# Attention scores in 32-query blocks on four column groups of TensorE, in a two-layer decoder trunk

## The chip, the cores and the metric

The kernel runs on one core of one Trainium2 chip. The metric is device time in microseconds (us) of one execution. A core has TensorE (PE, matmuls, with PEld its weight loads), VectorE (DVE), ScalarE (ACT), GpSimd (POOL) and SyncE (SP); each takes its instructions in program order, and semaphores order them among each other. Matmuls write PSUM, eight banks of 128 partitions x 2 KB; the other engines work between PSUM and SBUF.

## What is computed

Two layers of a decoder over 256 tokens of width 2048, each a mixer and a gated feed-forward network. Layer 0 mixes by gMLP and HGRN2, layer 1 by forgetting attention with 16 heads of 128. The change lies in the attention. What it must compute:

```python
def mixer_c(h, w_in, b_f, q_gain, k_gain, w_out):
    q, k, v, g, f = jnp.split(h @ w_in, ...)
    q = rms_norm(q.reshape(shp), q_gain)
    k = rms_norm(k.reshape(shp), k_gain)
    log_f = jax.nn.log_sigmoid(f + b_f)
    c = jnp.cumsum(log_f, axis=1).transpose(0, 2, 1)
    scale = C_HEAD_DIM ** -0.5
    for blk in range(seq // ATTN_BLOCK):          # two blocks of 128 queries
        lo, hi = blk * ATTN_BLOCK, (blk + 1) * ATTN_BLOCK
        s = jnp.einsum('bthd,bshd->bhts', q[:, lo:hi], k[:, :hi]) * scale
        s = s + c[:, :, lo:hi, None] - c[:, :, None, :hi]
        causal = (lo + jnp.arange(ATTN_BLOCK))[:, None] >= jnp.arange(hi)[None, :]
        p = jax.nn.softmax(jnp.where(causal, s, -jnp.inf), axis=-1)
        outs.append(jnp.einsum('bhts,bshd->bthd', p, v[:, :hi]))
    o = jnp.concatenate(outs, axis=1).reshape(bsz, seq, D_MODEL) * jax.nn.sigmoid(g)
    return o @ w_out
```

## The kernel before

All weights are streamed from HBM once, 484 MB in all. Every projection multiplies in split precision: a weight tile w of 128 x 1024 is loaded by SP's queue (L189), ACT rounds it to wh (L176), DVE takes the rest wl = w - wh (L177), and PE does three matmuls with 512 columns for each 128 x 512 part: L302 (wh), L303 (wl), L304 (wh with the low half of the activations) in the token-major projections, L321 to L323 in the feature-major ones. One tile feeds twelve matmuls. Four w, three wh and three wl buffers let the loads and halves run ahead. One call of tick() for each weight tile lets small generators (attend, gate, moves and so on) put their instructions between the projection's; a scheduler in the build then settles the order on each engine.

The attention's projections run in four groups of four heads: q, k and v of a group are three passes of project_tok over 16 parts of 128 features. The outputs of q and k are copied out of PSUM by ACT (z, L1051), squared and summed by DVE (junk L394, ss L395, then the reciprocal root: rm L386, a logarithm and an exponential on ACT L99, rt L389 to L391), scaled (L1059), transposed in 32 x 32 blocks by DVE (L334) and put in place by 16 DMAs of 32 KB, eight on SP's queue and eight on POOL's (L341, turn<-tmp).

Each pair of heads then goes through attend. ACT scales q and k into qk (L967). PE makes the scores of each head into one PSUM bank (L977, L978): queries 0 to 127 against keys 0 to 127, queries 128 to 255 against all 256; both are float32 matmuls, and what lies above the diagonal is computed and then masked. DVE adds the sums of the forget gates (ct by query, cb by key; L984, L986) and the mask cst (L988) and takes the maximum (L993); ACT takes the exponential and its sum (L99). DVE transposes the result in 32 x 32 blocks into ptmp (L1002), POOL's queue moves 16 blocks to pt (L1011), PE multiplies by v (L1023 to L1025) and ACT copies the two halves of the output to o, divided by the sums (L1027). At the end gate multiplies o with the sigmoid of the last projection's output.

PSUM: four banks (pm) hold the projections, four (px, through bank()) everything else. A matmul whose output lies in 32 partitions that start at 0, 32, 64 or 96 uses one of four column groups of the array. Three other places of the kernel do this already: L676 and L716 in the HGRN2 mixer, and L903 and L907 in the forget gates.

Of the kernel before, what the change touches and what calls it, by code (L numbers as in the profile page):

```python
# [8 lines left out]
F32 = mybir.dt.float32  # L9
F32R = mybir.dt.float32r  # L10
U16 = mybir.dt.uint16
AF = mybir.ActivationFunctionType
ALU = mybir.AluOpType
AX = mybir.AxisListType

P = 128
S = 256
# [3 lines left out]
CH = 16  # L21
# [3 lines left out]
BLK = 32  # L25
# [20 lines left out]
K_ID, K_TRI, K_CM, K_REV = 0, 128, 256, 384  # L46
# [8 lines left out]
def tile_trunk(ctx: ExitStack, tc: tile.TileContext, x, pp_d, cst_d, mlev_d, msk_d,  # L55
               w_v, w_f, w_g, w_i, w_q, w_u, w_abo, w_cf, w_cqkv, w_cg, w_co, w_up, w_dn, spw_d, spb_d, out):
    nc = tc.nc
    V, SC, PE = nc.vector, nc.scalar, nc.tensor
# [9 lines left out]
    def nm(base):  # L68
        count[0] += 1
        return f"{base}_{count[0]}"  # L70
# [3 lines left out]
    for c0, n in ((0, 1), (1, 1), (2, 2), (4, 2), (6, 2), (8, 4), (12, 4)):  # L74
        t = cp.tile([P, n, S], F32, tag=f"x{c0}", name=f"x{c0}")
# [4 lines left out]
    cst = cp.tile([P, NK], F32, tag="cst", name="cst")  # L80
# [30 lines left out]
    def turned(ap):  # L111

        return view(ap, 0, (1, 2), (2, P))

    def bank():
        return psum["pool"].tile([P, 512], F32, tag="px", name=nm("px"), bufs=psum["banks"])

    def banks(stack, n):

        psum.update(pool=stack.enter_context(tc.tile_pool(name=nm("px"), bufs=1, space=bass.MemoryType.PSUM)), banks=n)  # L120
        return psum["pool"]
# [243 lines left out]
    def held(r, last="wh"):  # L365

        tc.add_manual_dep(r.ins, deep[last].ins.name, order, reason="not before")
# [104 lines left out]
    def mixer_ab(norm):  # L472
        es = ExitStack()
        hp = es.enter_context(tc.tile_pool(name="hp", bufs=1))
# [161 lines left out]
        for j in range(2):  # L636
            ps = project_four(w_f[4 * j:4 * j + 4], A, KT)
# [3 lines left out]
            t = hp.tile([P, 1024], F32, tag="o", name=nm("turn"), bufs=2)  # L641
# [152 lines left out]
        for h in range(NH):  # L794
# [6 lines left out]
            ps = project(w_q[h], A)  # L801
# [5 lines left out]
        for j in range(2):  # L807
            ps = project_four(w_g[4 * j:4 * j + 4], A, KT)
# [16 lines left out]
        for j in range(2):  # L825
            ps = project_four(w_u[4 * j:4 * j + 4], A, KT)
# [3 lines left out]
            t = hp.tile([P, 1024], F32, tag="tok", name=nm("turn"), bufs=2)  # L830
# [12 lines left out]
        def stretch(q, ks, **kw):  # L843
            return project_four(w_abo[4 * q:4 * q + 4], product, KT, ks=ks, **kw)

        ahead = None
        for q in range(4):
            if q == 0:

                ps = stretch(0, (0, 2, 4, 6, 8, 10), more=True)  # L850
                ahead = stretch(1, (0, 2, 4, 6), more=True)
                stretch(0, (12, 14), ps=ps)
            elif q == 1:
                ps = stretch(1, (8, 10, 12, 14), ps=ahead)
            else:
                ps = stretch(q, range(0, KT, 2))
# [4 lines left out]
                depth[0] = 2  # L861
            add_four(q, ps, z, tmp, dst, nxt, 2 if q in (1, 2) else 1, (nc.sync, nc.gpsimd) if q else (nc.gpsimd,))
        es.close()
        banks(ctx, 4)
        return nxt


    def mixer_c(norm):
        es = ExitStack()
        hp = es.enter_context(tc.tile_pool(name="cpool", bufs=1))  # L870
# [23 lines left out]

        ct = hp.tile([P, 2, 2 * CH], F32, tag="ct", name="ct")[..., 0:CH]
        cb = hp.tile([P, CH * S], F32, tag="big", name="cb", bufs=1).rearrange("p (h s) -> p h s", s=S)

        def forget():

            ps = pm.tile([P, 512], F32, tag="pm", name=nm("pm"))  # L900
            pr = bank()
            for g in range(4):
                PE.matmul(pr[BLK * g:BLK * (g + 1), 0:LANE], ones[:, 0:BLK], norm.acc[:, LANE * g:LANE * (g + 1)],  # L903
                          start=True, stop=True)
            for k in range(KT):
                r = k % 4 * BLK
                PE.matmul(ps[r:r + CH, 0:S], w2[:, k], xT[k], start=k < 4, stop=k >= KT - 4, skip_group_check=True)  # L907
            return ps, pr
# [38 lines left out]
        def columns(fc):  # L947
            ps = bank()
            for T in range(2):
                PE.transpose(ps[:, T * P:(T + 1) * P], fc[:, T * P:(T + 1) * P], ident)  # L950
            V.tensor_copy(ct, ps[:, 0:S].rearrange("p (t c) -> p t c", t=2)[..., 0:CH])

        left = [CH]
        os_ = []
# [3 lines left out]
        def attend(hs, q, k, v, o):  # L958

            while steps[0] < turn[0]:  # L960
                yield
            turn[0] = steps[0] + PAIR
            qks = []
            for h in hs:
                qk = hp.tile([P, 2, S], F32, tag="qk", name=nm("qk"), bufs=2)
                for j, (t, g) in enumerate(((q, gq), (k, pp[:, C_KN:C_KN + 1]))):
                    r = SC.activation(qk[:, j].rearrange("p (t n) -> p t n", t=2), turned(t[:, h % 4]), AF.Copy, scale=g)  # L967
                    if j == 0:
                        held(r)
                qks.append(qk)  # L970
            yield
            sc = hp.tile([P, 6, P], F32, tag="sc", name=nm("sc"), bufs=1)
            scf = sc.rearrange("p a b -> p (a b)")
            sps = []
            for qk in qks:
                sp = bank()
                PE.matmul(sp[:, 0:P], qk[:, 0, 0:P], qk[:, 1, 0:P], start=True, stop=True)  # L977
                PE.matmul(sp[:, P:3 * P], qk[:, 0, P:S], qk[:, 1], start=True, stop=True)  # L978
                sps.append(sp)
            sums = []  # L980
            for i, (h, sp) in enumerate(zip(hs, sps)):
                c0 = 3 * P * i
                parts = ((c0, c0 + P), (c0 + P, c0 + 3 * P))
                V.scalar_tensor_tensor(scf[:, c0:c0 + P], sp[:, 0:P], ct[:, 0, h:h + 1], cb[:, h, 0:P],  # L984
                                       ALU.add, ALU.subtract)
                V.scalar_tensor_tensor(scf[:, c0 + P:c0 + 3 * P], sp[:, P:3 * P], ct[:, 1, h:h + 1], cb[:, h],  # L986
                                       ALU.add, ALU.subtract)
                V.tensor_tensor(sc[:, 3 * i:3 * i + 3:2], sc[:, 3 * i:3 * i + 3:2],  # L988
                                cst[:, K_CM:K_CM + P].unsqueeze(1).to_broadcast([P, 2, P]), ALU.add)
                mxs = hp.tile([P, LANE], F32, tag="mxs", name=nm("mxs"), bufs=2)[:, 0:2]  # L990
                sms = hp.tile([P, LANE], F32, tag="sms", name=nm("sms"), bufs=4)[:, 0:2]
                for T, (a, b) in enumerate(parts):
                    V.tensor_reduce(mxs[:, T:T + 1], scf[:, a:b], AX.X, ALU.max, negate=True)  # L993
                for T, (a, b) in enumerate(parts):
                    act(scf[:, a:b], scf[:, a:b], AF.Exp, bias=mxs[:, T:T + 1], accum_out=sms[:, T:T + 1])
                sums.append(sms)
            yield
            yield
            tmp = hp.tile([P, 6 * P], F32, tag="ptmp", name=nm("ptmp"), bufs=1)
            for i, sms in enumerate(sums):  # L1000
                V.reciprocal(sms, sms)
                t = V.transpose(tmp.rearrange("p (b m i) -> p b m i", b=4, m=6)[:, :, 3 * i:3 * i + 3],  # L1002
                                sc[:, 3 * i:3 * i + 3].rearrange("p m (b j) -> p b m j", b=4))
                if i == 0:
                    held(t, "wl")
            yield
            n = 6 * BLK
            pt = hp.tile([P, 6, P], F32, tag="pt", name=nm("pt"), bufs=2)
            for a in range(4):
                for b in range(4):  # L1010
                    nc.gpsimd.dma_start(pt[BLK * b:BLK * (b + 1), :, BLK * a:BLK * (a + 1)],  # L1011
                                        tmp[BLK * a:BLK * (a + 1), b * n:(b + 1) * n]
                                        .rearrange("p (m r) -> p m r", m=6))
                if a == 1:
                    yield
            for _ in range(LAG - 1):
                yield
            for i, (h, sms) in enumerate(zip(hs, sums)):
                d0 = (h % 4) * P
                op = bank()  # L1020
                v0, v1 = (v[:, T, d0:d0 + P] for T in range(2))
                p0, p1, p2 = (pt[:, 3 * i + m] for m in range(3))
                PE.matmul(op[:, 0:P], p0, v0, start=True, stop=True)  # L1023
                PE.matmul(op[:, P:S], p1, v0, start=True, stop=False)  # L1024
                PE.matmul(op[:, P:S], p2, v1, start=False, stop=True)  # L1025
                for T in range(2):
                    SC.activation(o[:, T, d0:d0 + P], op[:, T * P:(T + 1) * P], AF.Copy, scale=sms[:, T:T + 1])  # L1027
                left[0] -= 1

        def piece(tag, bufs):  # L1030
            return hp.tile([P, 1024], F32, tag=tag, name=nm(tag), bufs=bufs).rearrange("p (t c) -> p t c", t=2)
# [7 lines left out]
        for g in range(CH // 4):  # L1039
            qkv = []  # L1040
            ss = hp.tile([P, 2, 2, LANE // 4], F32, tag="ss", name=nm("ss"), bufs=2)[..., 0:4]
            for j in range(3):
# [5 lines left out]
                ps = early[j] if g == 0 and j < 2 else project_tok(w_cqkv[j * (CH // 4) + g], norm)  # L1048
# [6 lines left out]
                if j < 2:  # L1055
# [5 lines left out]
                    t = piece("turn", 4)  # L1061
# [34 lines left out]
        for q in range(CH // 4):  # L1096
            ps = project_four(w_cg[4 * q:4 * q + 4], A, KT)
# [6 lines left out]
        for q in range(4):  # L1104
            ps = project_four(w_co[4 * q:4 * q + 4], yB, KT)
# [236 lines left out]
```

## Time and profile before

| | |
|---|---|
| median of 3 runs | 2280.98 us (2280.97 to 2282.70) |
| the profiled execution | 2282.31 us, of which its span is 2280.5 us |
| attention stage with its projections | about 1120 to 1430 us of the span, the first scores at 1165.9 |
| PE busy between 1160 and 1430 us | 269.1 of 270.0 us |
| DVE, ACT, POOL busy between 1160 and 1430 us | 179.7, 149.9, 104.1 us |
| granted TensorE clock | 0.999 of full speed |

How to read the rows of the profile that follow. In a timeline a row has the start in us, the duration in us, the engine, the source line, the operation and the tiles (out<-in), the shape, and xN for N equal instructions that follow each other, merged; the brackets at the end tell how long the engine was idle before and what ended that. A float32 matmul stands as two PE records. The duration of a PE record includes its way through the array, so the distance between two starts, not the duration, tells how long PE was held. In a row of one line's instructions the three durations are minimum, median and maximum in ns. In the view of waits a row has the total in us, the number of times and the longest.

### The profile page before, as it was taken

The numbers are of one execution on the slowest core, as the hardware profiler recorded it, in microseconds if no ns is written. First come the engines' busy times: TensorE is split into PE (matmuls) and PEld (weight loads), VectorE is DVE, ScalarE is ACT, GpSimd is POOL, SyncE is SP. The second block draws the span as 40 slices with busy tenths as digits, with TensorE's granted clock in tenths as the row PEclk, the third lists the DMA queues.
The fourth block names the chain that finished last, engine by engine and source line by source line (L and its number), as shares of the span: only waits on it lengthen the run. The fifth ranks groups of instructions, "written<-read, shape, count | busy, mean of one in ns | idle before, by whom it ended". The sixth has DMA issues, their size and how long they took to land.

```text
span 2280.5 us, 32327 instructions
## 1 busy us (share of the span) xinstructions
PE 2273.4 (100%) x10786; PEld 1886.7 (83%) x10786; DVE 1562.2 (69%) x2301; ACT 1302.3 (57%) x1946; POOL 436.8 (19%) x798
## 2 busy tenths in 40 slices
PE   9999999999999999999999999999999999999999
PEld 8888888888888888888888888888888888888887
DVE  8788767767467656766876675666776476667766
ACT  7677656656456445654555556655665465455642
POOL 0120231221012002211233343211211012012102
PEclk9999999999999999999999999999999999999999
DMA  8655777777567666776676667777776676666766
GB/s 287 203 167 166 215 204 230 243 215 232 189 211 223 202 206 194 234 218 190 212 232 216 205 195 219 203 225 230 228 223 211 192 224 205 220 204 203 232 200 178
DMA packets 492615, 483.60 MB, mean 212 GB/s; under 512 B 115136, under 2 KB 460240, under 8 KB 492320
## 3 DMA queue, kind: packets, MB, share of 16 engines
q1 hardware_dynamic: 465888, 453.27, 64.1%
q0 software_dynamic: 24832, 25.92, 4.9%
q10 hardware_dynamic: 1728, 2.35, 0.3%
q8 instruction: 84, 1.38, 0.3%
q14 instruction: 83, 0.68, 0.1%
HBM read 435.24 MB, written 2.11 MB: 192 GB/s over the span
## 4 chain that ended last, share of the span: by engine, by line
PE 99%; DMA 1%; DVE 0%; issue 0%; POOL 0%; ACT 0%; DVEq 0%; SPq 0%
PE pm L321 27%; PE pm L323 27%; PE pm L322 27%; PE pm L302 4%; PE pm L303 4%; PE pm L304 4%; PE pm L276 2%; PE pm L203 1%; PE pm L279 1%; PE pm L227 0%; DMA pt<-ptmp 0%; PE px L978 0%; PE lv L716 0%; POOL pt L1011 0%; PE px L1024 0%
## 5 line engine op out<-in xcount | busy, mean ns | idle before, releaser
L177 DVE TENSOR_TENSOR wl<-w,wh 128x1024 fp32r<-128x1024 f32 (+1 forms) x820 | 995.9, 1218 | 611.7 <-ACT wh L176 580.6
L176 ACT ACTIVATE wh<-w 128x1024 fp32r<-128x1024 f32 (+1 forms) x820 | 862.7, 1054 | 763.1 <-PE pm L323 572.5
L321 PE MATMUL pm<-wh,a 128*128 128x512 f32 x1728 | 674.3, 390 | 0.0
L322 PE MATMUL pm<-wl,a 128*128 128x512 f32 x1728 | 672.6, 389 | 0.0
L323 PE MATMUL pm<-wh,a 128*128 128x512 f32 x1728 | 672.5, 389 | 0.0
L341 POOL DMA_DIRECT2D zt<-tmp x413 | 223.6, 549 | 1201.6 <-DVE tmp L334 1152.7
L323 PEld LDWEIGHTS pm<-wh,a 128*128 128x128 f32 x1728 | 324.4, 188 | 67.5
L321 PEld LDWEIGHTS pm<-wh,a 128*128 128x128 f32 x1728 | 324.4, 188 | 67.3
L322 PEld LDWEIGHTS pm<-wl,a 128*128 128x128 f32 x1728 | 324.4, 188 | 67.1 <-DVE wl L177 0.2
L323 PE MATMUL pm<-wh,hid 128*128 128x512 f32 x688 | 267.7, 389 | 0.0
L322 PE MATMUL pm<-wl,hid 128*128 128x512 f32 x688 | 267.7, 389 | 0.0
L321 PE MATMUL pm<-wh,hid 128*128 128x512 f32 x688 | 267.7, 389 | 0.0
L302 PE MATMUL pm<-wh,a 128*128 128x512 f32 x416 | 164.7, 396 | 0.0
L303 PE MATMUL pm<-wl,a 128*128 128x512 f32 x416 | 162.4, 390 | 0.9 <-DVE wl L177 0.9
L304 PE MATMUL pm<-wh,a 128*128 128x512 f32 x416 | 162.1, 390 | 0.0
L322 PEld LDWEIGHTS pm<-wl,hid 128*128 128x128 f32 x688 | 129.1, 188 | 26.8
L321 PEld LDWEIGHTS pm<-wh,hid 128*128 128x128 f32 x688 | 129.1, 188 | 26.8
L323 PEld LDWEIGHTS pm<-wh,hid 128*128 128x128 f32 x688 | 129.1, 188 | 26.8
L341 POOL DMA_DIRECT2D turn<-tmp x160 | 86.8, 550 | 316.7 <-DVE tmp L334 237.1
L1146 ACT ACTIVATE conv<-zt,pp 128x256 f32<-128x256 f32 x176 | 95.9, 590 | 36.1 <-DMA zt<-tmp 25.5
L1147 DVE SCALAR_TENSOR_TENSOR conv<-zt,pp,conv 128x255 f32<-128x255 f32 x176 | 79.7, 479 | 28.0 <-ACT conv L1146 27.7
L334 DVE STREAM_TRANSPOSE tmp<-z 128x512 f32<-128x512 f32 x120 | 82.8, 703 | 17.0 <-ACT z L1132 16.4
(246 smaller groups left out, 2131.6 us busy)
## 6 DMA issues: line engine op xcount, KB each, us to landing
w<-in_w_up SPq DMA_DIRECT2D x352, 512.0 KB, 4.9
w<-in_w_dn SPq DMA_DIRECT2D x176, 512.0 KB, 4.9
w<-in_w_cqkv SPq DMA_DIRECT2D x96, 512.0 KB, 4.6
w<-in_w_abo SPq DMA_DIRECT2D x32, 512.0 KB, 4.5
w<-in_w_cg SPq DMA_DIRECT2D x32, 512.0 KB, 4.6
w<-in_w_co SPq DMA_DIRECT2D x32, 512.0 KB, 4.8
zt<-tmp SPq DMA_DIRECT2D x414, 32.0 KB, 2.3
zt<-tmp POOLq DMA_DIRECT2D x413, 32.0 KB, 2.2
```

What stands on the lines that cost most here:

```text
L176: r = deep["wh"] = SC.activation(wh, w, AF.Copy)
L177: deep["wl"] = V.tensor_tensor(wl, w, wh.bitcast(F32), ALU.subtract)
L302: PE.matmul(ps[T], ah, h, start=k + i == 0, stop=False)
L303: PE.matmul(ps[T], ah, l, start=False, stop=False)
L304: deep["last"] = PE.matmul(ps[T], al, h, start=False, stop=k + i == KT - 1)
L321: PE.matmul(ps[T], ah, h, start=not begun and k + i == ks[0], stop=False)
L322: PE.matmul(ps[T], ah, l, start=False, stop=False)
L323: deep["mm"] = deep["last"] = PE.matmul(ps[T], al, h, start=False, stop=not more and k + i == ks[-1] + 1)
L334: V.transpose(tmp.rearrange("p (b m i t) -> p b m i t", b=4, m=4, t=2)[:, :, :, :, T], src(T).rearrange("p (m b j) -> p b m j", m=4, b=4))
L341: queues[(a + b) % len(queues)].dma_start(dst[BLK * b:BLK * (b + 1), :, a * n:(a + 1) * n], tmp[BLK * a:BLK * (a + 1), b * 4 * n:(b + 1) * ...
L1146: held(SC.activation(c, z, AF.Identity, bias=pp[:, cb:cb + 1], scale=w(2)))
L1147: V.scalar_tensor_tensor(c[:, 1:], z[:, :S - 1], w(1), c[:, 1:], ALU.mult, ALU.add)
```

## The change

The scores of a head are made in eight matmuls of 32 queries each in place of two of 128. Each block has only the keys up to its last query. The output partitions of a block decide its column group. The four blocks of the second 128 queries stand in order (groups 0 to 3 have 160, 192, 224, 256 keys), those of the first 128 back to front (groups 0 to 3 have 128, 96, 64, 32 keys). The scores get two PSUM banks of their own, cleared once, so that what is not computed is zero before the mask is added; the general banks go from four to two. Since the first half's queries now stand back to front by blocks of 32 in the partitions, the mask (causal) and the query's gate sums (ct) are made in that order, and the output copies turn them back: four copies of 32 partitions and one of 128 in place of two of 128 for each head. The probabilities' way through ptmp, pt and the product with v stays as it was.

```diff
@@ mixer_ab
-        banks(ctx, 4)
+        banks(ctx, 2)
@@ mixer_c
+        causal = hp.tile([P, 2, P], F32, tag="causal", name="causal")
+        scores = es.enter_context(tc.tile_pool(name="sx", bufs=1, space=bass.MemoryType.PSUM))
+        sps = [scores.tile([P, 512], F32, tag=f"sp{i}", name=f"sp{i}") for i in range(2)]
+        for sp in sps:
+            V.memset(sp[:, 0:3 * P], 0.0)
+
+        def facing(a):
+            return slice(BLK * a, BLK * (a + 1)), slice(BLK * (3 - a), BLK * (4 - a))
+
+        SC.activation(causal[:, 1], cst[:, K_CM:K_CM + P], AF.Copy)
+        for a in range(4):
+            to, at = facing(a)
+            SC.activation(causal[to, 0], cst[at, K_CM:K_CM + P], AF.Copy)
@@ columns
-            V.tensor_copy(ct, ps[:, 0:S].rearrange("p (t c) -> p t c", t=2)[..., 0:CH])
+            V.tensor_copy(ct[:, 1], ps[:, P:P + CH])
+            for a in range(4):
+                to, at = facing(a)
+                V.tensor_copy(ct[to, 0], ps[at, 0:CH])
@@ attend
-            sps = []
-            for qk in qks:
-                sp = bank()
-                PE.matmul(sp[:, 0:P], qk[:, 0, 0:P], qk[:, 1, 0:P], start=True, stop=True)
-                PE.matmul(sp[:, P:3 * P], qk[:, 0, P:S], qk[:, 1], start=True, stop=True)
-                sps.append(sp)
+            for sp, qk in zip(sps, qks):
+                for T in range(2):
+                    for a in range(4) if T == 0 else reversed(range(4)):
+                        q0 = P + BLK * a if T else BLK * (3 - a)
+                        n, c = q0 + BLK, T * P
+                        PE.matmul(sp[BLK * a:BLK * (a + 1), c:c + n], qk[:, 0, q0:q0 + BLK], qk[:, 1, 0:n],
+                                  start=True, stop=True)
...
-                                cst[:, K_CM:K_CM + P].unsqueeze(1).to_broadcast([P, 2, P]), ALU.add)
+                                causal, ALU.add)
...
-                for T in range(2):
-                    SC.activation(o[:, T, d0:d0 + P], op[:, T * P:(T + 1) * P], AF.Copy, scale=sms[:, T:T + 1])
+                for a in range(4):
+                    at, to = facing(a)
+                    SC.activation(o[to, 0, d0:d0 + P], op[at, 0:P], AF.Copy, scale=sms[at, 0:1])
+                SC.activation(o[:, 1, d0:d0 + P], op[:, P:S], AF.Copy, scale=sms[:, 1:2])
```

In the changed kernel the output copies stand at L1045 and L1046, the score matmuls at L995.

## The prediction, made before the changed kernel ran

> **What bounds the kernel now.** I read the page first, then the timeline of PE around the scores, the timelines of ACT and DVE behind them, and last the timeline of PE at the three other places where the kernel already works in column groups.
>
> ```profile
> span 2280.5 us, 32327 instructions
> PE 2273.4 (100%) x10786; PEld 1886.7 (83%) x10786; DVE 1562.2 (69%) x2301; ACT 1302.3 (57%) x1946; POOL 436.8 (19%) x798
> PE 99%; DMA 1%; DVE 0%; issue 0%; POOL 0%; ACT 0%; DVEq 0%; SPq 0%
> ```
>
> PE has work in all but 7 us of the span and is 99% of the chain that ended last. So the time moves by two things only: how long PE is held by the scores, and whether PE has to wait for weight halves (wh from ACT, wl from DVE) that come later than now. Everything else is hidden.
>
> **What the scores cost PE now.** The timeline of PE at the first pair of heads:
>
> ```profile
> 1165.23 0.39 PE L302 MATMUL pm<-wh,a 128*128 128x512 f32 x1
> 1165.45 0.39 PE L303 MATMUL pm<-wl,a 128*128 128x512 f32 x1
> 1165.68 0.39 PE L304 MATMUL pm<-wh,a 128*128 128x512 f32 x1
> 1165.91 0.38 PE L977 MATMUL px<-qk 128*128 128x128 f32 x2
> 1166.13 0.60 PE L978 MATMUL px<-qk 128*128 128x256 f32 x2
> 1166.56 0.38 PE L977 MATMUL px<-qk 128*128 128x128 f32 x2
> 1166.78 0.60 PE L978 MATMUL px<-qk 128*128 128x256 f32 x2
> 1167.03 0.58 PE L302 MATMUL pm<-wh,a 128*128 128x512 f32 x1
> 1167.45 0.40 PE L303 MATMUL pm<-wl,a 128*128 128x512 f32 x1
> ```
>
> Projection matmuls start 0.227 us apart (1165.23 to 1165.68 is two). From the L304 at 1165.68 to the L303 at 1167.45 are 1.77 us, in which only two such slots lie (0.45): the scores of two heads hold PE for 1.32 us. They run without a seam: a float32 matmul stands as two records, and the two of 256 keys take 1166.13 to 1166.56, 0.215 us each, those of 128 keys half of it, 0.84 ns for each key and record. A head has 128 + 256 = 384 keys, twice: 0.65 us. There are eight pairs, 10.5 us in all. That is all that the scores can give.
>
> **What they cost afterwards.** A head becomes eight blocks of 32 queries: 128, 96, 64, 32 keys for the first half (column groups 0 to 3) and 256, 224, 192, 160 for the second (groups 3 to 0). That is 1152 keys; one after another they would take 1152 x 2 x 0.84 = 1.94 us. But each column group gets 288 (128+160, 96+192, 64+224, 32+256), so if the four run side by side a head takes 288 x 2 x 0.84 = 0.49 us, and a pair 0.97. What switching to column groups and back costs is in two places that exist already:
>
> ```profile
> 107.33 0.39 PE L279 MATMUL pm<-a,wl 128*128 128x256 f32 x2
> 107.65 0.43 PE L676 MATMUL px<-kq 128*32 128x64 f32 x16
> 108.01 0.73 PE L276 MATMUL pm<-a,wh 128*128 128x512 f32 x2
> 108.58 0.39 PE L279 MATMUL pm<-a,wl 128*128 128x256 f32 x2
> 108.81 0.62 PE L276 MATMUL pm<-a,wh 128*128 128x512 f32 x2
> 109.28 0.40 PE L279 MATMUL pm<-a,wl 128*128 128x256 f32 x2
> ...
> 1138.74 0.39 PE L304 MATMUL pm<-wh,a 128*128 128x512 f32 x1
> 1139.06 0.32 PE L903 MATMUL px<-acc,ones 128*32 128x64 f32 x8
> 1139.20 1.91 PE L907 MATMUL pm<-x,w 128*16 128x256 f32 x32
> 1141.04 0.50 PE L302 MATMUL pm<-wh,a 128*128 128x512 f32 x1
> 1141.37 0.39 PE L303 MATMUL pm<-wl,a 128*128 128x512 f32 x1
> ```
>
> The 32 records of L907 have 256 keys' worth of columns each; alone they would take 32 x 0.215 = 6.9 us, and they take 1.91 less the tail of the last: 8 rounds of 0.215, 1.72 us. So four groups do run side by side, at full speed. Now the switch. L279 to L279 is 0.70 us undisturbed (108.58 to 109.28) and 1.25 with L676 between: 0.55, of which 16 records of 64 columns in four groups are 4 x 0.054 = 0.22. Left for the way in and out: 0.33. In the other place, L304 to L303 is 2.63, less two slots 0.45, less 1.72 for L907 and two rounds of 64 for L903 (0.11): 0.35. I take 0.34, once for each pair, since both heads' scores follow each other. A pair then costs 0.97 + 0.34 = 1.31 against 1.32 now. **PE gains nothing**: what the mask saves, the switch takes back. Bounds for this step: if the way in and out were hidden, 8 x 0.34 = 2.7 us faster; above, see the rivals.
>
> One assumption is not covered by equal blocks: that a short block lets its group go on to the next one while a longer one still runs. The nearest rows:
>
> ```profile
> 131.08 0.61 PE L716 MATMUL lv<-E 128*32 128x32 f32 x47
> 131.51 0.24 PE L716 MATMUL px<-E 128*32 128x64 f32 x1
> 131.52 0.20 PE L716 MATMUL lv<-E 128*32 128x32 f32 x1
> ```
>
> The px block is later in the program than the last lv record, and starts 0.01 us before it: groups are not held to the program's order, at least over one place. The Trainium skill, "TensorE: Matmul & The Clock Gate", part 3 (packing small matmuls), says that tiles overlap but that matmuls start and end strictly in order. By that rule each round lasts as long as its longest block, which is the second rival; these rows speak against the start half of it, and say nothing of ends of unequal blocks. "TensorEngine Tiling (Array Packing)", instruction overhead, in the Trainium skill, says a matmul of one column costs as much as one of 60; by its figure the 32-key block would add, as an estimate, some 0.05 us a head, 0.7 us in all, but 48 lv records in 131.08 to 131.52 (0.009 us each, four at a time) are shorter than it allows, so I add nothing.
>
> **What moves on ACT and DVE.** The output copies at L1027 go from two to five a head (four of 32 partitions, since the first 128 queries must be turned back), 48 more in all. A pair's ten stand in a row on ACT in the built kernel's order, where four stood:
>
> ```profile
> 1197.05 0.21 ACT L99 ACTIVATE ss<-rm 128x8 f32<-128x8 f32 x1 [5.36 <-DVE rm L386]
> 1197.17 1.04 ACT L176 ACTIVATE wh<-w 128x1024 fp32r<-128x1024 f32 x1
> 1198.12 0.19 ACT L99 ACTIVATE ss<-ss 128x8 f32<-128x8 f32 x1
> ...
> 1212.29 1.06 ACT L176 ACTIVATE wh<-w 128x1024 fp32r<-128x1024 f32 x1 [4.48 <-DMA w<-in_w_cqkv]
> 1213.25 1.13 ACT L1027 ACTIVATE o<-px,sms 128x128 f32<-128x128 f32 x4
> 1214.25 1.28 ACT L1051 ACTIVATE z<-pm,Rt 128x512 f32<-128x512 f32 x2
> ...
> 1217.83 1.22 DVE L177 TENSOR_TENSOR wl<-w,wh 128x1024 fp32r<-128x1024 f32 x1
> 1223.20 2.32 DVE L177 TENSOR_TENSOR wl<-w,wh 128x1024 fp32r<-128x1024 f32 x2
> ...
> 1293.21 2.31 DVE L177 TENSOR_TENSOR wl<-w,wh 128x1024 fp32r<-128x1024 f32 x2
> ...
> 1219.11 0.50 PE L303 MATMUL pm<-wl,a 128*128 128x512 f32 x1
> 1224.67 0.39 PE L303 MATMUL pm<-wl,a 128*128 128x512 f32 x1
> 1295.67 0.39 PE L303 MATMUL pm<-wl,a 128*128 128x512 f32 x1
> ```
>
> Four copies take 1.00 us to the z behind them, 0.25 each. A copy of 32 partitions has as many elements in each as one of 128, so I price it the same: six more are 1.5 us. (From below, L721's copy of 64 elements takes 0.215 against 0.362 for L1027, which would make 0.9; from above, six unoverlapped at 0.36 make 2.2.)
>
> ```profile
> L721 ACT ACTIVATE st<-px x16: 201/215/222, 133.3 to 229.7; 64x64 f32<-64x64 f32 x16
> ```
>
> Who waits: behind the second pair of each group stand the two z (L1051), behind these the junk and ss of the key norm on DVE, and in DVE's order wl copies for PE. Against the 1.5 us stands a gain: for the first pair the built order has the wh of 1197.17 ahead of the logarithm, so the exponential need not wait for it (0.6 us), nor the wl behind it on DVE, and the norm's transposes come some 1.2 us earlier. Their eight moves stand ahead of the weight loads on SP's queue, and it is a weight load that the wh at 1212.29 waits for (its releaser); so all after it starts 1.2 earlier and the z are 0.3 us late. DVE's order also puts one wl ahead of the second reduction, so the wl of 1217.83 is no later and the wait before the L303 at 1219.11 (0.33 after its L302 instead of 0.227, and the next L304 as late: 0.2) goes. But the norm's end now has two wl copies ahead of it instead of one, so the transposes and the wl at 1223.20 come some 0.9 us later: it ends at 1225.3, and L303 wants it at 1224.67. That is a wait of 0.7 and 0.1 for the reload of weights. In the next group the same wl has 1.3 us of cover (1293.21 + 1.2 against 1295.67), enough for 0.9. The later transposes delay the moves and the loads behind them in group 0 by 0.9 against 0.6 that PE lost: 0.2 more.
>
> Hidden: five copies for the mask at the start and four more for ct (once; ACT and DVE are 57% and 69% busy); the two memsets of the score banks (on DVE, long before, between two links that wait for ACT); the banks going from four to two, as two heads' outputs use two and the next pair comes 60 projection matmuls (13.6 us) later; the DMA issues on POOL, which are the same. If ACT had no idle time the 48 copies would cost 12 us.
>
> **Sum.** PE 8 x (1.31 - 1.32), nothing, and 0.2 for seams between unequal blocks; waits -0.2 + 0.8 + 0.2 = 0.8; together +1.0 us. The profiled execution took 2282.31 us (span 2280.5 and 1.8 around it), 1.3 above the median of the runs shown, 2280.98. I put the sum on the median: **2282.0 us**, own range 2280.5 to 2285. What a measurement of this kernel tells from no change is about 0.2%, 4.6 us; so the forecast is no change.
>
> **Rivals.**
> A, the copies come through: ten in a row delay z by 1.5 us, the early moves do not help, and the delay reaches PE in full in groups 0, 1 and 2 and for about 1.0 behind the last pairs, where the gates' sigmoids and a weight load stand behind the copies too. 3 x 1.5 + 1.0 = 5.5 us: 2286.5, slower. It decides once the delay passes the 1.3 us of cover in group 1. For it: PE waits for wl already now, at 1219.11. Against: most wl have more cover, as 99% of the chain is PE.
> B, rounds in step: a round ends with its longest block, 128 then 256 keys. A head is 384 keys again, a pair 1.30 + 0.34; 8 x 0.32 = 2.6 us on top: 2284.6.
> C, program order holds groups back further, so that on average two of four run: 1152 / 2 x 2 x 0.84 = 0.97 a head, 2.28 a pair, 8 x 0.96 = 7.7 us: 2289.7. L907 speaks against it, with equal blocks.
> D, the change does more than I grant: the way in and out overlaps (-2.7), and with it the waits of PE for wl that stand in this stage now go:
>
> ```profile
> PEld pm L303 <- DVE wl L177: 2.1, 3, 1.3
> ```
>
> 2280.98 - 2.7 - 2.1 = 2276.2. Against it: both places above show the 0.34 in full, and the longest of these waits, 1.3, comes before the first output copy.
>
> **How the numbers follow.** Forecast 0.40, A 0.22, B 0.16, C 0.10, D 0.12. Range 2278 to 2289: it takes A and B whole and leaves out most of C and the further half of D. Slower by over 0.2% (above 2285.5): most of A (0.20), a third of B (0.05), C (0.10), 0.01 of the forecast: 0.36. Faster (below 2276.4): two thirds of D, 0.08. Same: 0.56.
>
> **What would show it.** Right: a pair's scores hold PE for 1.3 us between the L304 ahead and the second projection matmul behind, with records of one group starting before a longer neighbour ends; each L1045 copy about 0.25 us apart; at 1223 to 1226 one wait of PE for wl of under a microsecond. B shows as rounds of four that start together, 0.1 and 0.2 us apart; C as starts of neighbours far apart; A as waits of PE for wl over 1 us behind each second pair. I am wrong if the eight pairs together change by more than 3 us, or if copies of 32 partitions cost much more than 0.25.

## The result and the profile after

| | before | after |
|---|---|---|
| median | 2281.85 us (2280.70 to 2282.70) | 2284.80 us (2283.68 to 2286.88) |
| the profiled execution | 2282.31 us, span 2280.5 | 2283.68 us, span 2281.9 |

The ratio after to before is 1.0015, with a 95% interval of 1.0009 to 1.0021: 2.95 us more, inside the 0.2% that the prediction calls no change, on the side of slower. The profiled execution of before is among the longer ones of its kernel, that of after is the shortest of its kernel, so their spans differ by less than the medians do.

The page of after, its first row, the busy row and the shares of the chain that ended last:

```profile
span 2281.9 us, 32772 instructions
PE 2274.9 (100%) x10978; PEld 1882.8 (83%) x10978; DVE 1563.2 (69%) x2307; ACT 1322.7 (58%) x1999; POOL 436.9 (19%) x798
PE 97%; ACT 1%; DVE 1%; issue 0%; DMA 0%; POOL 0%; SPq 0%; DVEq 0%; ACTq 0%
```

PE is still the bound, but the chain now leaves it and goes through ACT and DVE for 2% of the span: PE waits for something that these two were late with. ACT is busy 20.4 us longer (1302.3 before).

**The scores.** The timeline of PE at the first pair of heads, after:

```profile
1165.94 0.39 PE L303 MATMUL pm<-wl,a 128*128 128x512 f32 x1
1166.17 0.39 PE L304 MATMUL pm<-wh,a 128*128 128x512 f32 x1
1166.49 1.20 PE L995 MATMUL sp<-qk 128*32 128x128 f32 x32
1167.62 0.50 PE L302 MATMUL pm<-wh,a 128*128 128x512 f32 x1
1167.96 0.40 PE L303 MATMUL pm<-wl,a 128*128 128x512 f32 x1
```

From 1166.17 to 1167.96 are 1.79 us; less two slots of 0.227 the pair holds PE for 1.33 us (by the unrounded starts 1.333, at each of the eight pairs). Before it was 1.313. So the eight pairs cost 8 x 0.020 = 0.16 us more: the mask's saving and the switch cancel.

**The output copies.** The timeline of ACT behind the second pair of heads, after:

```profile
1208.82 1.06 ACT L176 ACTIVATE wh<-w 128x1024 fp32r<-128x1024 f32 x1 [1.66 <-PE pm L304]
1209.90 1.48 ACT L1045 ACTIVATE o<-px,sms 32x128 f32<-32x128 f32 x4
1211.39 0.37 ACT L1046 ACTIVATE o<-px,sms 128x128 f32<-128x128 f32 x1
1211.77 1.47 ACT L1045 ACTIVATE o<-px,sms 32x128 f32<-32x128 f32 x4
1213.25 0.37 ACT L1046 ACTIVATE o<-px,sms 128x128 f32<-128x128 f32 x1
1213.52 1.26 ACT L1070 ACTIVATE z<-pm,Rt 128x512 f32<-128x512 f32 x2
```

Four copies take 1.48 us, 0.37 each. Before, four copies of 128 partitions took 1.00 us to the z behind them because each began 0.11 us before the one ahead had ended. Here each of the first nine ends before the next begins. The ten take 3.62 us (1209.90 to 1213.52) where four took 1.00.

**Who waits for them.** The timeline of DVE, after, where the brackets give its idle time and what ended it:

```profile
1214.23 0.69 DVE L394 TENSOR_TENSOR junk<-z 128x512 f32<-128x512 f32 x1 [3.10 <-ACT z L1070]
...
1221.72 1.30 DVE L334 STREAM_TRANSPOSE tmp<-z 128x512 f32<-128x512 f32 x2
1222.94 3.46 DVE L177 TENSOR_TENSOR wl<-w,wh 128x1024 fp32r<-128x1024 f32 x3
...
1429.19 1.29 DVE L1097 TENSOR_TENSOR z<-z,o 128x512 f32<-128x512 f32 x2 [4.20 <-ACT z L99]
1430.40 1.30 DVE L334 STREAM_TRANSPOSE tmp<-z 128x512 f32<-128x512 f32 x2
1431.63 3.46 DVE L177 TENSOR_TENSOR wl<-w,wh 128x1024 fp32r<-128x1024 f32 x3
```

And PE, after, at the four places where these wl are wanted:

```profile
1223.57 0.39 PE L302 MATMUL pm<-wh,a 128*128 128x512 f32 x1
1224.18 0.50 PE L303 MATMUL pm<-wl,a 128*128 128x512 f32 x1 [0.22 <-DVE wl L177]
1224.51 0.39 PE L304 MATMUL pm<-wh,a 128*128 128x512 f32 x1
...
1295.47 0.50 PE L303 MATMUL pm<-wl,a 128*128 128x512 f32 x1 [0.22 <-DVE wl L177]
...
1366.76 0.50 PE L303 MATMUL pm<-wl,a 128*128 128x512 f32 x1 [0.22 <-DVE wl L177]
...
1432.00 0.39 PE L321 MATMUL pm<-wh,a 128*128 128x512 f32 x1
1432.87 0.50 PE L322 MATMUL pm<-wl,a 128*128 128x512 f32 x1 [0.48 <-DVE wl L177]
```

DVE stands still for 3.1 us until the first z is out. The norm's chain, its transposes and the three wl that have piled up behind them come late. The first of the three begins at 1222.94, takes 1.2 us, and PE starts its L303 at 1224.18, 0.61 us after the L302 instead of 0.23; the L304 behind it comes 0.11 late as well. That is 0.49 us lost, and it recurs in each of the first three groups (1224, 1295, 1367). Behind the last pairs the z wait for the gates' product instead, and PE loses 0.75. Together 3 x 0.49 + 0.75 = 2.2 us. With the 0.16 of the scores that makes 2.4, against 2.3 by which the span differs from that of an execution of before without waits (2279.6, below).

### The profile page after: what moved, and what is told of

It is laid out like the page before. It is cut to its first block, busy times and chain, and to the rows that moved or that the text cites. A ratio compares the mean times of both kernels' runs of the same rounds, so it can differ in the third digit from the quotient of the medians.

```text
span 2281.9 us, 32772 instructions
## 1 busy us (share of the span) xinstructions
PE 2274.9 (100%) x10978; PEld 1882.8 (83%) x10978; DVE 1563.2 (69%) x2307; ACT 1322.7 (58%) x1999; POOL 436.9 (19%) x798
## 4 chain that ended last, share of the span: by engine, by line
PE 97%; ACT 1%; DVE 1%; issue 0%; DMA 0%; POOL 0%; SPq 0%; DVEq 0%; ACTq 0%
PE pm L321 26%; PE pm L322 26%; PE pm L323 26%; PE pm L302 4%; PE pm L303 4%; PE pm L304 4%; PE pm L203 1%; PE pm L276 1%; PE pm L279 1%; ACT o L1045 0%; PE pm L227 0%; DVE wl L177 0%; PE sp L995 0%; ACT wh L176 0%; PE lv L716 0%
## 5 line engine op out<-in xcount | busy, mean ns | idle before, releaser
L302 PE MATMUL pm<-wh,a 128*128 128x512 f32 x416 | 164.2, 395 | 0.0
L303 PE MATMUL pm<-wl,a 128*128 128x512 f32 x416 | 162.5, 391 | 0.7 <-DVE wl L177 0.7
L304 PE MATMUL pm<-wh,a 128*128 128x512 f32 x416 | 162.0, 389 | 0.0
```

The lines of the kernel that those rows point to most:

```text
L302: PE.matmul(ps[T], ah, h, start=k + i == 0, stop=False)
L303: PE.matmul(ps[T], ah, l, start=False, stop=False)
L304: deep["last"] = PE.matmul(ps[T], al, h, start=False, stop=k + i == KT - 1)
```

## The experiments

My theory after these readings: the time goes to the output copies. A copy whose first partition differs from that of the copy ahead does not overlap it, ten in a row make z late, and PE waits for wl at four places. Rivals: the waits come from the new order of instructions or the two general PSUM banks, which the scores bring; they come with the number of copies, whatever their partitions; or they are chance and come in either kernel. For the scores: groups that go on independently, against rounds in step and against program order.

**The copies alone** (e1_copies): the kernel before, with the first half's output copy cut into four, each to the partitions that it came from.

```diff
-                for T in range(2):
-                    SC.activation(o[:, T, d0:d0 + P], op[:, T * P:(T + 1) * P], AF.Copy, scale=sms[:, T:T + 1])
+                for a in range(4):
+                    at = slice(BLK * a, BLK * (a + 1))
+                    SC.activation(o[at, 0, d0:d0 + P], op[at, 0:P], AF.Copy, scale=sms[at, 0:1])
+                SC.activation(o[:, 1, d0:d0 + P], op[:, P:S], AF.Copy, scale=sms[:, 1:2])
```

> The kernel before, with its scores as they were, and only the output copy of the first 128 queries cut into four copies of 32 partitions, each to the partitions it comes from. Theory 1 (the copies cost the 3 us): 10 copies in a row take 3.7 us as in the changed kernel (0.37 from start to start, where four of 128 partitions took 0.25 each), z comes 2.7 us later behind the second pair of a group, PE waits for wl there, and the kernel is 2 to 3 us slower than before. If the 0.37 comes from the turning to other partitions and not from the 32 partitions, the copies are 0.25 apart here and the loss is under 1 us. Theory 2 (the blocks of scores, their switch and the fewer banks cost it): no change, within 0.5 us.

Measured: 2284.54 us against 2281.09, ratio 1.0015 (1.0006 to 1.0023), 3.45 us more where the theory had 2 to 3: the whole loss of the change with none of its scores. The timeline of ACT in this kernel:

```profile
1210.20 1.47 ACT L1028 ACTIVATE o<-px,sms 32x128 f32<-32x128 f32 x4
1211.68 0.37 ACT L1029 ACTIVATE o<-px,sms 128x128 f32<-128x128 f32 x1
1211.95 1.46 ACT L1028 ACTIVATE o<-px,sms 32x128 f32<-32x128 f32 x4
```

The same 0.37 apart. The copy of 1211.95 follows that of 1211.68 after 0.27, not 0.37: it starts at partition 0 as the one ahead does. PE's waits in the view of waits are of the same kind, and by the starts they stand at the places of the change (1224, 1297, 1368, 1434) and at one more, 1290, 3.6 us in all:

```profile
PEld pm L303 <- DVE wl L177: 3.7, 4, 1.2
PEld pm L322 <- DVE wl L177: 0.6, 1, 0.6
```

**The scores alone** (e2_scores): the change with two copies; the first half of the output stays back to front, so the output is not the reference's.

```diff
-                for a in range(4):
-                    at, to = facing(a)
-                    SC.activation(o[to, 0, d0:d0 + P], op[at, 0:P], AF.Copy, scale=sms[at, 0:1])
-                SC.activation(o[:, 1, d0:d0 + P], op[:, P:S], AF.Copy, scale=sms[:, 1:2])
+                for T in range(2):
+                    SC.activation(o[:, T, d0:d0 + P], op[:, T * P:(T + 1) * P], AF.Copy, scale=sms[:, T:T + 1])
```

> The changed kernel with two output copies a head as before; it leaves out the turning, so the first 128 queries of each head come out back to front by blocks of 32. Theory 1: a pair's scores hold PE for 1.33 us against 1.31, 0.2 us in all, and the kernel is within 0.5 us of the one before. Theory 2: 2 to 3 us slower, as the changed kernel.

Measured: 2281.54 us, ratio 1.0002 (0.9993 to 1.0011), span 2279.7. A pair holds PE for 1.333 us as in the change, and PE waits nowhere for wl between 1160 and 1440. The timeline of DVE shows the cover that the copies had used up:

```profile
1219.82 1.30 DVE L334 STREAM_TRANSPOSE tmp<-z 128x512 f32<-128x512 f32 x2
1221.04 2.50 DVE L177 TENSOR_TENSOR wl<-w,wh 128x1024 fp32r<-128x1024 f32 x2
```

and that of PE where the first of these is wanted:

```profile
1223.96 0.39 PE L303 MATMUL pm<-wl,a 128*128 128x512 f32 x1
```

The first wl is done 1.25 us after 1221.04, at 1222.3, and the L303 that takes it starts at 1223.96: 1.7 us of cover. In the change the wl starts 1.9 us later (1222.94) while PE is 0.16 us earlier: 2.06 against 1.67 leaves the wait of 0.38 that stands there.

The scheduler in the build orders DVE's work in the change otherwise than here, one wl ahead of the norm's second sum, so that order could be a cause too. It is a small one: from the first junk to the transposes are 7.49 us in the change and 7.40 here (7.14 in the second profile of before, below), while the z starts 1.8 us later (1213.52 against 1211.70). So neither the order nor the two general banks bring the waits; the copies do.

**The two heads apart** (e4_apart): the scores alone, with the second head's scores one weight tile behind the first's, so that PE switches sixteen times; one waiting step behind them is taken out to keep the length. The first half again stays back to front.

```diff
             for sp, qk in zip(sps, qks):
+                if qk is qks[1]:
+                    yield
...
-            yield
             yield
```

> As the run of the scores alone (two output copies, first 128 queries left back to front), but the second head's scores one weight tile later than the first's, so that PE goes into the column groups and out again 16 times in place of 8; one of the two steps of waiting behind them is taken out. If a switch costs 0.34 us, each head holds PE for 0.49 + 0.34 = 0.83 us and the kernel is 8 x 0.34 = 2.7 us slower than the scores alone. If the switch is hidden or the 0.34 is something else (a tail of the last record, say, that lies beside other work), under 1 us slower.

Measured: 2299.25 us, ratio 1.0082 (1.0070 to 1.0095). Each head's scores hold PE for 0.832 us, 0.49 of work and 0.34 of switch, as priced: 8 x (2 x 0.832 - 1.333) = 2.65 us for the eight added switches. The rest is mostly a wait that I had made myself. In the timeline of PE and the view of waits:

```profile
1216.18 0.77 PE L1041 MATMUL px<-v,pt 128*128 128x128 f32 x2 [6.01 <-DMA pt<-ptmp]
```
```profile
PE px L1041 <- DMA pt<-ptmp: 10.5, 2, 6.0
```

Twice PE comes to the product with v before pt has been moved: these two products hold PE for 8.9 and 7.2 us instead of 1.343. Of the 13.5 us more, 10.5 are waiting; in the other 3.0 the matmuls stand further apart, and the granted clock is 0.50 from 1216.18 to 1218.70 and 0.58 from 1293.74 to 1296.00. Whether the step less behind the scores or the second head's later scores makes pt late was not separated. The price of the switch stands; the total says nothing of it.

**Natural order** (e5_forward): no turning, no extra copies; groups 0 to 3 have 32 + 160, 64 + 192, 96 + 224 and 128 + 256 keys.

```diff
-            return slice(BLK * a, BLK * (a + 1)), slice(BLK * (3 - a), BLK * (4 - a))
+            return slice(BLK * a, BLK * (a + 1)), slice(BLK * a, BLK * (a + 1))
...
-                    for a in range(4) if T == 0 else reversed(range(4)):
-                        q0 = P + BLK * a if T else BLK * (3 - a)
+                    for a in reversed(range(4)):
+                        q0 = P * T + BLK * a
...
```

> Blocks of 32 queries in four column groups, but the first 128 queries in their own order (32, 64, 96, 128 keys in groups 0 to 3) like the second 128: no turning, two output copies, and the output is right. Group 3 gets 128 + 256 = 384 keys a head, so a pair should hold PE for 2 x 384 x 2 x 0.84 ns + 0.34 = 1.63 us against 1.31, and the kernel be 2.6 us slower than before. If work of the next head in the other groups hides the long group, or a round's shorter blocks do not let their group go on, the time of a pair does not follow the longest group: 1.33 as back to front (then no slower than before).

Measured: 2283.35 us, ratio 1.0010 (1.0001 to 1.0019), span 2281.4, no waits of PE for wl. The timeline of PE at the first pair:

```profile
1166.00 0.39 PE L304 MATMUL pm<-wh,a 128*128 128x512 f32 x1
1166.32 1.49 PE L995 MATMUL sp<-qk 128*32 128x128 f32 x32
1167.73 0.50 PE L302 MATMUL pm<-wh,a 128*128 128x512 f32 x1
1168.07 0.40 PE L303 MATMUL pm<-wl,a 128*128 128x512 f32 x1
```

A pair takes 1.62 us (1168.07 - 1166.00 - 0.454; 1.619 by the unrounded starts). That is 0.33 and 2 x 384 x 2 x 0.84 ns = 1.29, the sum of the longest group: it sets the time. Back to front the longest has 288 keys, which gives 0.97 + 0.34 = 1.31 and 1.333 measured. A round that ended with its longest block would make 1.63 in both orders. Turning therefore does save 8 x 0.286 = 2.3 us on PE, and the waits behind the copies that turn back take 2.2 in the first profile of the change and 3.6 in e1_copies.

**The kernel before, once more** (e6_before), unchanged.

> The kernel before, unchanged, for a second profile. In the first profile PE waits 1.2 us for wl at 1191.7, 0.2 at 1219 and 0.3 at 1235, yet that execution (2282.31) is among the slower of its runs (2280.70 to 2282.70). If these waits come and go with the landing of the pt moves, this profile lacks the one at 1191 and its span is about 1 us shorter; then the changed kernel's extra waits are 2 us and more beside it. If the waits belong to the kernel, they stand here again, and 1.5 of the 3 us between the medians have no place in the profiles. Time: the same as before within 0.3 us.

Measured: 2281.03 us, ratio 0.9999 (0.9989 to 1.0008), span 2279.6, and no wait of PE for wl in this stage. The profile of before that the prediction was made from has three, 1.7 us by the starts, the longest at 1191.68. The timeline of DVE in that first profile shows where it is from:

```profile
1189.95 0.58 DVE L1002 STREAM_TRANSPOSE ptmp<-sc 128x384 f32<-128x384 f32 x1 [3.91 <-DMA pt<-ptmp]
1190.45 1.18 DVE L177 TENSOR_TENSOR wl<-w,wh 128x1024 fp32r<-128x1024 f32 x1
```

DVE waits 3.91 us for an earlier move out of ptmp to land, and the wl that PE wants stands behind it. In the second profile DVE waits 0.95 us there, and PE not at all: this wait comes and goes with the landing of those moves. The two shorter ones, 0.2 at 1219.11 and 0.3 at 1235.72, come behind it and are gone with it.

**The change, once more** (e8_again), unchanged.

> The changed kernel, unchanged, for a second profile. Its first profile (2283.68) is the fastest of its 21 runs. Expected here: the scores 1.33 us a pair again, output copies 0.37 apart, waits of PE for wl near 1224, 1295, 1367 and 1433 of 0.5 us or more, 1 to 2 us more of them in all than the 2.2 of the first profile. Time: 2.5 to 3.5 us over the kernel before.

Measured: 2284.48 us, ratio 1.0016 (1.0007 to 1.0025); the profiled execution, 2286.48 us with a span of 2284.7, is the longest of its ten runs, as the first profile was the shortest of its own. Its waits of PE:

```profile
PEld pm L303 <- DVE wl L177: 5.5, 6, 1.4
PEld pm L322 <- DVE wl L177: 0.9, 1, 0.9
```

And the one DVE row ahead of the longest of them, and the wh ahead of the output copies on ACT:

```profile
1190.87 0.58 DVE L1019 STREAM_TRANSPOSE ptmp<-sc 128x384 f32<-128x384 f32 x1 [4.03 <-DMA pt<-ptmp]
...
1211.56 1.06 ACT L176 ACTIVATE wh<-w 128x1024 fp32r<-128x1024 f32 x1 [2.83 <-DMA w<-in_w_cqkv]
```

By the starts PE loses 5.3 us, 3.1 more than in the first profile, where 1 to 2 more were expected. Of that 1.3 come behind the DVE row, at 1192.61, as in the first profile of before, and 0.7 at 1173.58, ahead of any output copy, where DVE had waited 3.73 us for a move of the gate sums (cb<-cd). The places of the first profile stand here again (1226.93, 1298, 1370, 1436) and lose 2.8. The remaining 0.6, at 1220.38, is at the place of the 0.2 at 1219.11 in the first profile of before.

The trace also shows why 1226.93 loses 1.1 where 1224 lost 0.5. The wh ahead of the copies waits for its weight load, as it did in the first profile of before (1212.29), and starts 2.75 us later than in the first profile of the change. So does the wl that PE wants (1225.69 against 1222.94). PE is only 2.15 later there, so the wait is 0.6 longer. Without such an early wait before loses nothing and the change 2.2; with one, before loses 1.7 and the change 5.3. That is one profile for each.

**As many copies, one first partition** (e9_columns): the kernel before, with the first half's copy cut into four by columns, 128 x 32 each.

```diff
-                for T in range(2):
-                    SC.activation(o[:, T, d0:d0 + P], op[:, T * P:(T + 1) * P], AF.Copy, scale=sms[:, T:T + 1])
+                for c in range(0, P, BLK):
+                    SC.activation(o[:, 0, d0 + c:d0 + c + BLK], op[:, c:c + BLK], AF.Copy, scale=sms[:, 0:1])
+                SC.activation(o[:, 1, d0:d0 + P], op[:, P:S], AF.Copy, scale=sms[:, 1:2])
```

> The kernel before with the output copy of the first 128 queries cut into four, as in the run of the copies alone, but by columns: each of 128 partitions and 32 columns, so that no copy starts at another partition than the one ahead. If it is the change of the first partition that keeps a copy from overlapping with the next (0.37 apart, where 128 partitions after 128 partitions were 0.25 apart), these copies stand 0.25 apart or less, ten of them take 2.5 us at most, and the kernel is less than 0.7 us slower than before. If any further copy costs its 0.37, 3.7 us for the ten and 2.5 to 3.5 us slower, as with the copies by partitions.

Measured: 2281.03 us, ratio 1.0000 (0.9991 to 1.0009), no waits for wl. The timeline of ACT:

```profile
1210.84 0.80 ACT L1027 ACTIVATE o<-px,sms 128x32 f32<-128x32 f32 x4
1211.52 0.38 ACT L1028 ACTIVATE o<-px,sms 128x128 f32<-128x128 f32 x1
1211.77 0.85 ACT L1027 ACTIVATE o<-px,sms 128x32 f32<-128x32 f32 x4
1212.45 0.43 ACT L1028 ACTIVATE o<-px,sms 128x128 f32<-128x128 f32 x1
1212.69 1.34 ACT L1052 ACTIVATE z<-pm,Rt 128x512 f32<-128x512 f32 x2
```

Four are 0.68 us to the one behind them, 0.17 each, though each lasts 0.27 to 0.34 us: they overlap. Ten take 1.85 us. The number of copies is not it. These copies are also shorter; that the first partition and not the length decides is seen in e1_copies, where 32 x 128 overlaps behind a copy of the same first partition and not behind another.

**Two halves exchanged** (e7_halves): the first 128 queries turned by blocks of 64 and not 32. Groups 0 to 3 hold 96, 128, 32, 64 keys of the first half, so the longest has 128 + 192 = 320; the copies are two of 64 partitions and one of 128.

```diff
+        H = P // 2
         def facing(a):
-            return slice(BLK * a, BLK * (a + 1)), slice(BLK * (3 - a), BLK * (4 - a))
+            return slice(H * a, H * (a + 1)), slice(H * (1 - a), H * (2 - a))
...
-                        q0 = P + BLK * a if T else BLK * (3 - a)
+                        q0 = P + BLK * a if T else BLK * (a ^ 2)
...
```

> The changed kernel with the two halves of the first 128 queries exchanged in place of the four blocks turned (groups 0 to 3 hold 96, 128, 32, 64 keys): three output copies a head (64, 64, 128 partitions) in place of five. The longest groups get 320 keys a head, so a pair should hold PE 2 x 320 x 2 x 0.84 ns + 0.35 = 1.43 us, 0.9 us over the eight pairs. Six copies in a row at 0.37 are 2.2 us against 1.0 before and 3.7 changed, so z comes 1.2 us later than before. If the delay of z must pass some 1.5 us before PE waits, no waits and 1.0 to 1.5 us slower than before in all; if waits grow in step with the copies, 0.9 + 1.2 = 2.1 us or more.

Measured: 2281.61 us, ratio 1.0003 (0.9994 to 1.0012), no waits for wl. A pair holds PE for 1.419 us, where 320 keys make 1.08 + 0.34. The timeline of ACT:

```profile
1210.21 0.74 ACT L1047 ACTIVATE o<-px,sms 64x128 f32<-64x128 f32 x2
1210.96 0.37 ACT L1048 ACTIVATE o<-px,sms 128x128 f32<-128x128 f32 x1
1211.34 0.74 ACT L1047 ACTIVATE o<-px,sms 64x128 f32<-64x128 f32 x2
1212.09 0.37 ACT L1048 ACTIVATE o<-px,sms 128x128 f32<-128x128 f32 x1
1212.35 0.68 ACT L1072 ACTIVATE z<-pm,Rt 128x512 f32<-128x512 f32 x1
```

0.37 apart again, but six and not ten: 2.14 us in all, 1.1 more than before, which the cover holds. The kernel is 0.6 us over before, where the expectation had 1.0 to 1.5. Among the kernels tried that compute the reference with column groups this is the shortest, and not told from the kernel before.

No kernel here beats the one before. Two ways were not tried: turning the first half back without ACT's copies, and letting two pairs of heads share one switch, which by the 0.34 would save an estimated 4 x 0.34 = 1.4 us, less than a comparison here tells.

## Why the prediction was right and where it was not

The forecast of no change held: 1.0015 is inside 0.2%, and 2284.80 inside the range, above the forecast's own 2282.0. The scores bear it out; the account of the copies does not. Copies that "cost much more than 0.25" were the prediction's own sign of being wrong, and they cost 0.37. That the total stayed inside 0.2% all the same is in part luck: the band is wide against the 1.0 us forecast, and the cover in front of PE took most of the delay.

**The scores: right, in mechanism and size.** 1.31 predicted, 1.333 measured; 0.2 for seams predicted, 0.16 measured in all. The switch of 0.34 is seen again: less the longest group's keys, a pair of 288, 320 and 384 keys (1.333, 1.419, 1.619) leaves 0.37, 0.34 and 0.33, and one head (0.832) 0.35, any seams included. Rivals B and C fall with it: B needed 1.64 for a pair in both orders, C 2.28. The records of one head begin like this in the trace of after (start, duration in us as modelled, keys of the block; each matmul twice):

```
1166.490 0.297  128     1166.563 0.196   32 (second record)
1166.497 0.270   96     1166.584 0.219   64 (second record)
1166.504 0.243   64     1166.595 0.382  256
1166.510 0.217   32     1166.604 0.246   96 (second record)
```

The block of 256 keys, fifth in the program, starts ahead of the second record of the block of 96 keys, which is second: each group goes on when its own block has left.

The Trainium skill, "TensorE: Matmul & The Clock Gate", part 3, says that matmuls start and end strictly in program order. For these groups the starts above are out of order; the ends are too, but only as the profile models them (the 32-key block's second record at 1166.76, the 128-key block's first at 1166.79). What does not rest on modelled ends is the 1.333 us for a pair, where rounds in step would take 1.64.

**The copies: the term that was mis-sized.** The prediction priced a copy of 32 partitions "the same" as one of 128 in a row, 0.25, and six more at 1.5 us, with 2.2 as its bound from above for six unoverlapped. It measured 0.37 each, and not only the six new ones: nine of the ten do not overlap the one behind them, and only the last overlaps the z. So the ten take 2.6 us more than four (3.62 - 1.00), beyond even that bound, which left out that the four already there lose their overlap too. The row that would have told stood in the trace of before, in another place of the same operation. The group of L917, four small copies, each from another first partition, all to the same one:

```profile
L917 ACT ACTIVATE Rf<-Rq x4: 238/254/256, 1150.5 to 1151.3; 16x64 f32<-16x64 f32 x4
```

Minimum, median and maximum duration are 238, 254 and 256 ns; the starts, 1150.502, 1150.751, 1151.019 and 1151.285, are 0.25 to 0.27 apart, so no two overlap.

**The gain set against them: partly right.** The wh ahead of the copies did start earlier, at 1208.82 in place of 1212.29 in the first profile of before, and no longer waits for a weight load there. But most of that was not the change's: the second profile of before has the same wh at 1210.01, and PE's wait at 1191.68, behind which the first profile was late, is missing there. Against the scores alone (1209.66) the gain is 0.84, where 1.2 was predicted. So the z come 1.8 us late (1213.52 against 1211.70) and not 0.3, and the transposes 1.9 (1221.72 against 1219.82) and not 0.9: the new order on DVE, which the prediction held for most of its 0.9, adds 0.1.

**The waits: right in kind, wrong in number and size.** One wait of 0.7 and 0.1 in group 0 was predicted; 0.38 and 0.11 stands there in one profile and more in the other. Group 1 was to be covered: the delay was 2.1 us and not 0.9, the cover 1.7 and not 1.3, so groups 1 and 2 lose as much as group 0. The gates' end was left out of the sum and has the longest wait in the first profile, 0.64 and 0.11. In total +0.8 predicted; at these places 2.2 and 2.8 measured, in the two profiles.

**Rival A** is what happened in mechanism: the copies come through in every group and behind the last pairs. Its price, 5.5 us, took the delay as 1.5 and the loss as the whole of it; in fact the delay is over 2 and PE loses what passes the cover. Its sign, waits over 1 us behind each second pair, stands at one place only, 1226.93 in the second profile of the change.

**Rival D** was right in one point only, that the wait at 1191 could go: it is absent in the first profile of after, but also in the second of before, and it stands in the second of after, so it was no gain.

## What to carry to other kernels

Before a full-height instruction is cut into pieces by partitions, look in the trace for pieces of that engine that change their first partition, and take the distance between their starts as the price, for the old pieces of the row too; by columns the same cut cost a third (0.85 us in place of 2.6). A serial row on an engine with idle time costs nothing until it passes the cover of what waits behind it: measure that cover (wanted minus ready) at each place, and in more than one execution, because a wait in a single profile may be chance, and such a wait takes cover away. Column groups of TensorE cost, in this kernel, the sum of the longest group plus about a third of a microsecond for the way in and out, so balance the groups and put as many blocks as possible behind one switch.

## What the runs showed that I had not expected

- ACT's copies overlap the one ahead by 0.10 us or more if they keep the first partition (0.169 apart at 0.27 to 0.34 long, e9_columns) and not at all if it changes (0.37 apart at 0.36 long). The side that is written counts as well as the one that is read: in after the L1045 of 1211.77 reads from partition 0 as the L1046 ahead of it does, but writes from 96, and comes 0.38 behind it; L917 changes only the side that it reads. The Trainium skill, "ScalarE: Activation LUTs", What ACT_TABLE_LOAD costs, says, of tiles with 128 partitions, that back-to-back ACTIVATEs overlap by about 93 ns, and names no condition on the first partition; copies of the first kind here overlap by that and more, those of the second not at all.
- Column groups with unequal blocks run on independently, close to full speed: 1.333, 1.419 and 1.619 us for a pair with 288, 320 and 384 keys in the longest group, where 0.84 ns for each key and record and one switch of 0.34 make 1.31, 1.42 and 1.63.
- Moving the second head's scores by one weight tile and taking out one waiting step behind them costs 13.5 us at two products with v (e4_apart), 10.5 of them waiting for the moves of pt.
